# Order edges between bank additions, weight sums and gated sums in a convolutional FFN kernel

## The chip, the cores and the metric

The kernel runs on one core of a Trainium2 chip. Time is device time in microseconds of one launch. Before the change the median of three runs is 2473.03 us (2470.02 to 2473.74).

## The reference

A two-layer decoder on a 1024 x 1024 float32 activation: first an RG-LRU mixer, then a stick-breaking attention, each followed by a convolutional FFN (`D_FF` = 3072) and a layer norm. The change touches the FFN alone:

```python
def causal_depthwise_conv(x, w, b):
    ...
    y = b + xp[:, 0:S] * w[0]
    for k in range(1, K):
        y = y + xp[:, k:k + S] * w[k]
    return y

def conv_ffn(x, w_up, conv_w, conv_b, w_down):
    h = causal_depthwise_conv(x @ w_up, conv_w, conv_b)
    return (jax.nn.gelu(h[..., :D_FF]) * h[..., D_FF:]) @ w_down
```

## The kernel before, in words

**Matmuls.** Every float32 operand is split into a high half (a cast on ACT, tile `whi`, L90) and a low half (a subtraction on POOL, tile `wlo`, L96, on DVE where asked for), and each product takes three matmuls, high by high, high by low, low by high.

**Up projection** (`up`, up to `down` at 866 us in the first layer and at 2213 us in the second). The 24 blocks of 128 hidden units are taken one after the other; block j has a gate half and a value half, 128 x 1024 each. Blocks 0 and 1 are plain. Blocks 2 to 23 use seven half-size products instead of eight (`seven`), with sums of weights (s1 to s4, `combine`, DVE, L467) and sums of the activations made once. PE runs the products in this order: w11 into the bank `cv`, w1 into a bank `p` of its own, w2 on top of w11, w12 into `cg`, then w3, w4, w22. Between them ACT copies banks (L591 `cg<-cv`, L593 `p5s<-p`, L601 `cv<-cv`) and DVE makes two bank additions: c12 (L598, `cg<-cv,p5s`) and c22 (L602, `cv<-cv,p5s`). A product that adds onto such a half waits for its addition. The next block's w11 is started with four matmuls ahead of w3, its other eight stand behind w22.

When both banks are full, `activate` convolves them: ACT scales by the last tap (L483), DVE adds the two other taps in one instruction each (L485), ACT takes the gelu (L491), DVE multiplies the halves (L493, "mul" here).

**Gated sums.** The down projection is also made of seven products for the first 18 blocks. `store(j)` of an odd j makes four sums of the gated halves of the blocks j - 1 and j on POOL (L513, L515, L517, L519) and stores seven half tiles to device memory on SP's queue; it is called while block j + 1 is set up, so the gated sums run in the even blocks 2 to 18. The weight sums and three of the gated sums share one pool tag, `s`, with four buffers. A tag `t2`, four buffers too, is used at the start of the stage alone.

**Down projection** (`down`, `sevens`). Gated half tiles are read back (`graw`, L693, four buffers), weights are loaded (`wr`, L669), the differences T1 to T4 of weights are made on DVE (L675), both operands are split, PE multiplies (L699) and DVE adds the results to the residual `xres` (L650, L653). The first eight operands have their low halves on POOL, of later ones every third is DVE's.

**What sets the order.** A scheduler arranges the instructions of each engine; the engine then runs its list strictly in order, each instruction waiting on semaphores for what it needs. An instruction whose input is ready can so stand behind one that waits. Loads and stores of this stage stand in SP's list, with the same rule. `tc.issue_after(x)` adds an edge: what is issued under it, on x's engine, stands behind x.

Of the kernel before, what the change touches and what calls it, by code (L numbers as in the profile page):

```python
# [7 lines left out]
F32 = mybir.dt.float32  # L8
# [46 lines left out]
def trunk(tc, a):  # L55
# [3 lines left out]
    with ExitStack() as outer:  # L59
# [28 lines left out]
        def split_sb(hi, lo, src, hi_eng="act", lo_eng="pool"):  # L88
            if hi_eng == "act":
                A.copy(out=hi, in_=src)  # L90
            elif hi_eng == "dve":
                V.tensor_copy(out=hi, in_=src)
            else:
                G.tensor_scalar(out=hi, in0=src, scalar1=1.0, scalar2=0.0, op0=ALU.mult, op1=ALU.add)
            eng = G if lo_eng == "pool" else V
            eng.tensor_tensor(out=lo, in0=src, in1=hi.bitcast(F32), op=ALU.subtract)  # L96

# [320 lines left out]
        def ffn(layer, last):  # L418

            gd = [[dram.tile([P, HS], F32, name=f"gs{layer}_{m}_{i}") for i in range(7)] for m in range(NSEV // 2)]  # L420
            gd += [dram.tile([P, S], F32, name=f"gd{layer}_{j}") for j in range(NSEV, NFF)]
            up(layer, last, gd)
            down(layer, last, gd)

        def up(layer, last, gd):
# [6 lines left out]
            with ExitStack() as ph:  # L432
# [18 lines left out]
                def operand(src):  # L451
                    w = Split(ring.tile([P, HS], F32R, name="whi", tag="whi"),
                              ring.tile([P, HS], F32R, name="wlo", tag="wlo"))
                    split_sb(w.hi, w.lo, src)
                    return w

                def blocks(j):

                    out = {}
                    for f, k in ((0, 0), (1, 0), (1, 1), (0, 1)):  # L460
                        raw = out[f, k] = rawp[j % 2].tile([P, HS], F32, name="wraw", tag="wraw")
                        nc.sync.dma_start(out=raw, in_=a["w_up"][layer, f * NFF + j][:, k * HS:(k + 1) * HS])
                    return [out[f, k] for f in range(2) for k in range(2)]
# [25 lines left out]
                def activate(j, pg, pu):  # L489
                    ug = conv(pg, j, "ug", 2)  # L490
                    A.activation(out=ug, in_=ug, func=AF.Gelu_apprx_tanh)  # L491
                    uv = conv(pu, NFF + j, "uv", 1)
                    V.tensor_tensor(out=ug, in0=ug, in1=uv, op=ALU.mult)  # L493
                    done.append(ug)
# [3 lines left out]
                def store(j):  # L498
# [4 lines left out]
                    elif j % 2:  # L503
                        a11, a21, a12, a22 = two(done[j - 1]) + two(done[j])
                        s1, s2, s4 = (sums.tile([P, HS], F32, name="s", tag="s") for _ in range(3))

# [68 lines left out]
                def seven(j, raws):  # L575
                    r11, r12, r21, r22 = raws
                    (b11, b12), (b21, b22) = xq
                    t1, t2, t3, t4 = Ts
                    s1 = combine(ALU.add, r21, r22)
                    s2 = combine(ALU.subtract, s1, r11)  # L580
                    s3 = combine(ALU.subtract, r11, r21)
                    s4 = combine(ALU.subtract, r12, s2)
                    w11, w1, w2, w12, w3, w4, w22 = (operand(r) for r in (r11, s1, s2, r12, s3, s4, r22))
# [17 lines left out]
                    A.copy(out=c21, in_=c22)  # L601
                    V.tensor_tensor(out=c22, in0=c22, in1=p5s, op=ALU.add)  # L602
                    product(c21, w22, t4, False, True)
# [3 lines left out]
                for j in range(NFF):  # L607
                    raws, nxt = nxt, blocks(j + 1) if j + 1 < NFF else None
                    if j in PLAIN:
                        ps = plain(j, raws, None if j else PAIRS if last else (0, 1, 2, 3))  # L610
                        if j == 0:
                            sums_of_x((0, 2, 1))
                    else:
                        ps = seven(j, raws)
                    if j:
                        store(j - 1)
                    activate(j, *ps)
                store(NFF - 1)

        def sevens(layer, gd, ph, banks):  # L620
# [16 lines left out]
            def operand(src, name):  # L637
                w = Split(ring.tile([P, HS], F32R, name=name + "h", tag=name + "h"),
                          ring.tile([P, HS], F32R, name=name + "l", tag=name + "l"))
                turns[0] += 1  # L640
                split_sb(w.hi, w.lo, src, lo_eng="dve" if turns[0] > 8 and turns[0] % 3 == 0 else "pool")
                return w
# [12 lines left out]
            for group, m0 in enumerate(range(0, NSEV // 2, GROUP)):  # L655
                B = {}
                wrp = wrps[group % 2]

                def weight(n, m):
# [6 lines left out]
                    if n in ("11", "12", "21", "22"):  # L666
                        k, d = int(n[0]) - 1, HALVES[int(n[1]) - 1]
                        out = (wfp if n == "11" else wrp).tile([P, HS], F32, name="wr", tag="wr")
                        nc.sync.dma_start(out=out, in_=a["w_down"][layer, (2 * m + k) * P:(2 * m + k + 1) * P, d])  # L669
# [34 lines left out]

        def down(layer, last, gd):
            with ExitStack() as ph:
# [16 lines left out]
                pend = Ends()  # L723
                with ExitStack() as ph7:
                    sevens(layer, gd, ph7, (pmid, pend))
# [323 lines left out]
```

## Time and profile before

| | us |
|---|---|
| median of three runs | 2473.03 |
| the profiled execution, time | 2473.08 |
| its span | 2471.4 |
| layer 0: up projection, blocks 2 to 22 | 435.95 |
| layer 1: the same | 436.92 |

Granted TensorE clock over the span: 0.982 of full speed. The span starts with the RG-LRU mixer; the FFN of layer 0 ends at 1072 us, the attention of layer 1 runs from there to 1713, and its FFN to the end. A row of a timeline gives start and length of an instruction (several of a kind in a row are joined, with xN), and in brackets how long its engine was idle before it and what it waited for. `cv<-Th,whi` is a matmul into bank `cv`.

### The profile page before, as it was taken

Reading aid. Unit: us, or ns where it says so; the run is one execution under the profiler, and the core shown is the slowest. Engines: PE = TensorE matmul, PEld = TensorE weight load, DVE = VectorE, ACT = ScalarE, POOL = GpSimd, SP = SyncE. Lnnn points to the kernel's source line nnn. Section 1 sums busy time; section 2 is a strip of 40 time slices with the busy share of each in tenths; the row PEclk is TensorE's granted clock in tenths of the full one; section 3 lists DMA queues with packets and bytes.
Section 4 is the critical chain, followed back from the end, with each engine's and each line's share of the span. In section 5 each row is a group of like instructions: output and inputs, shape, how many; then the busy total and the mean of one; then the engine's idle time right before and its main releaser. Section 6 shows DMA issues by size and latency. Waiting matters only on the chain.

```text
span 2471.4 us, 29325 instructions
## 1 busy us (share of the span) xinstructions
PE 2306.7 (93%) x10708; PEld 1886.2 (76%) x10708; DVE 1533.0 (62%) x1722; ACT 1004.3 (41%) x1571; POOL 1334.2 (54%) x954
## 2 busy tenths in 40 slices
PE   8999979999999989999999999988999999989998
PEld 6877768777777778888877788767777777768787
DVE  5694756565656578763466555685656565657866
ACT  4644234444444434423433334343444444444441
POOL 4686365565655466764323223246565655456675
PEclk9999989999999999999999999998999999999999
DMA  6111022232322353411011011002222222235351
GB/s 219 47 54 51 18 73 73 81 107 86 105 84 96 106 174 109 147 52 52 26 35 34 26 35 35 26 18 81 77 98 95 93 99 87 90 109 168 103 175 68
DMA packets 95184, 204.52 MB, mean 83 GB/s; under 512 B 10560, under 2 KB 12224, under 8 KB 95040
## 3 DMA queue, kind: packets, MB, share of 16 engines
q1 hardware_dynamic: 90144, 187.74, 23.2%
q10 hardware_dynamic: 4896, 14.92, 1.7%
q8 instruction: 84, 1.38, 0.2%
q14 instruction: 60, 0.49, 0.1%
HBM read 159.10 MB, written 43.52 MB: 82 GB/s over the span
## 4 chain that ended last, share of the span: by engine, by line
PE 56%; DVE 11%; issue 10%; POOL 6%; ACT 1%; DMA 0%; POOLq 0%; DVEq 0%; ACTq 0%
PE cv L475 16%; PE po L699 11%; PE cg L475 5%; PE p L475 5%; DVE s L467 2%; PE pp L114 2%; DVE e L891 2%; PE pp L115 2%; PE pp L116 2%; PE po L153 2%; PE po L154 2%; PE po L157 2%; DVE wr L675 1%; DVE xres L862 1%; POOL s L513 1%
## 5 line engine op out<-in xcount | busy, mean ns | idle before, releaser
L96 POOL TENSOR_TENSOR wlo<-wraw,whi 128x512 fp32r<-128x512 f32 (+2 forms) x217 | 382.4, 1766 | 373.3 <-ACT whi L90 358.1
L96 POOL TENSOR_TENSOR wlo<-s,whi 128x512 fp32r<-128x512 f32 x176 | 233.2, 1330 | 235.8 <-ACT whi L90 183.0
L90 ACT CAST whi<-wraw 128x512 fp32r<-128x512 f32 (+2 forms) x209 | 146.1, 703 | 302.9 <-PE cv L475 126.8
L90 ACT CAST whi<-s 128x512 fp32r<-128x512 f32 x176 | 109.2, 621 | 340.5 <-PE cg L475 117.3
L699 PE MATMUL po<-wh,gh 128*128 128x512 f32 x504 | 198.3, 395 | 23.2 <-DVE ug L485 18.8
L699 PE MATMUL po<-wl,gh 128*128 128x512 f32 x504 | 198.0, 393 | 0.0
L699 PE MATMUL po<-wh,gl 128*128 128x512 f32 x504 | 198.0, 393 | 0.0
L96 POOL TENSOR_TENSOR gl<-graw,gh 128x512 fp32r<-128x512 f32 x86 | 123.9, 1443 | 111.9 <-ACT gh L90 103.7
L475 PE MATMUL cv<-Th,whi 128*128 128x512 f32 x352 | 143.6, 408 | 25.8 <-DVE cg L598 25.3
L475 PE MATMUL cv<-xTh,whi 128*128 128x512 f32 x352 | 139.0, 395 | 25.7 <-DVE cv L602 25.7
L467 DVE TENSOR_TENSOR s<-wraw 128x512 f32<-128x512 f32 x88 | 116.4, 1323 | 70.3 <-POOL wlo L96 67.4
L90 ACT CAST gh<-graw 128x512 fp32r<-128x512 f32 x126 | 78.4, 622 | 190.5 <-PE po L699 68.4
L485 DVE SCALAR_TENSOR_TENSOR ug<-cg,pv,ug 128x1023 f32<-128x1023 f32 x88 | 112.6, 1280 | 49.3 <-ACT ug L483 47.8
L114 PE MATMUL pp<-xTh,whi 128*128 128x512 f32 x352 | 143.1, 406 | 0.0
L475 PE MATMUL cv<-Th,wlo 128*128 128x512 f32 x352 | 137.9, 392 | 0.0
L116 PE MATMUL pp<-xTh,wlo 128*128 128x512 f32 x352 | 137.9, 392 | 0.0
L475 PE MATMUL cv<-Tl,whi 128*128 128x512 f32 x352 | 137.9, 392 | 0.0
L115 PE MATMUL pp<-xTl,whi 128*128 128x512 f32 x352 | 137.8, 391 | 0.0
L475 PE MATMUL cg<-xTh,whi 128*128 128x512 f32 x352 | 137.3, 390 | 0.0
L475 PE MATMUL cg<-xTh,wlo 128*128 128x512 f32 x352 | 137.1, 390 | 0.0
L475 PE MATMUL cv<-xTl,whi 128*128 128x512 f32 x352 | 137.1, 389 | 0.0
L475 PE MATMUL cg<-xTl,whi 128*128 128x512 f32 x352 | 137.0, 389 | 0.0
(254 smaller groups left out, 6448.1 us busy)
## 6 DMA issues: line engine op xcount, KB each, us to landing
wraw<-in_w_up SPq DMA_DIRECT2D x192, 256.0 KB, 2.6
graw<-gs SPq DMA_DIRECT2D x126, 256.0 KB, 2.9
wr<-in_w_down SPq DMA_DIRECT2D x72, 256.0 KB, 4.4
gs<-ug SPq DMA_DIRECT2D x72, 256.0 KB, 2.4
gs<-s SPq DMA_DIRECT2D x54, 256.0 KB, 2.0
wraw<-in_w_in SPq DMA_DIRECT2D x14, 512.0 KB, 3.6
mraw<-gd SPq DMA_DIRECT2D x12, 512.0 KB, 4.3
draw<-in_w_down SPq DMA_DIRECT2D x12, 512.0 KB, 4.5
```

Source lines behind the costliest of these rows:

```text
L90: A.copy(out=hi, in_=src)
L96: eng.tensor_tensor(out=lo, in0=src, in1=hi.bitcast(F32), op=ALU.subtract)
L114: T.matmul(out, lhsT=l.hi, rhs=r.hi, start=start, stop=False)
L115: T.matmul(out, lhsT=l.hi, rhs=r.lo, start=False, stop=False)
L116: T.matmul(out, lhsT=l.lo, rhs=r.hi, start=False, stop=stop)
L153: T.matmul(po[h], lhsT=g.hi, rhs=w.hi[:, d], start=st, stop=False)
L154: T.matmul(po[h], lhsT=g.hi, rhs=w.lo[:, d], start=False, stop=False)
L157: T.matmul(po[h], lhsT=g.lo, rhs=w.hi[:, d], start=False, stop=sp)
L467: V.tensor_tensor(out=s, in0=x, in1=y, op=op)
L475: T.matmul(ps, lhsT=l, rhs=r[:, c, :], start=start and c == k == 0, stop=stop and c == 3 and k == 2, skip_group_check=True)
L485: V.scalar_tensor_tensor(out=u[:, k:], in0=ps[:, :S - k], scalar=cw[:, 2 - k:3 - k], in1=u[:, k:], op0=ALU.mult, op1=ALU.add)
L699: T.matmul(acc[c][t], lhsT=l, rhs=r, start=not on and m == m0 and k == 0, stop=m == m0 + GROUP - 1 and k == 2, skip_group_check=True)
```

## The change

1. `split_sb` returns its last instruction, and `up` keeps a few instructions in `mark`: the last low half, the last load, the last c22, the last mul.
2. The weight sums of a block are issued behind the c22 addition of the block before (an edge on DVE).
3. `store(j - 1)` is issued behind the last low half (POOL) and the last load (SP).
4. The gated sums take tiles of tag `t2`, so that tag `s` has the weight sums and the short use at the start alone.
5. `sevens` is issued behind the last mul. The first twelve operands have their low halves on POOL. The weight pools are dealt out anew: "21" always from one, "12" and "22" from the other in turn.

```diff
@@ -93,7 +93,7 @@
             else:
                 G.tensor_scalar(out=hi, in0=src, scalar1=1.0, scalar2=0.0, op0=ALU.mult, op1=ALU.add)
             eng = G if lo_eng == "pool" else V
-            eng.tensor_tensor(out=lo, in0=src, in1=hi.bitcast(F32), op=ALU.subtract)
+            return eng.tensor_tensor(out=lo, in0=src, in1=hi.bitcast(F32), op=ALU.subtract)
 
         stage = {}
 
@@ -419,8 +419,7 @@
 
             gd = [[dram.tile([P, HS], F32, name=f"gs{layer}_{m}_{i}") for i in range(7)] for m in range(NSEV // 2)]
             gd += [dram.tile([P, S], F32, name=f"gd{layer}_{j}") for j in range(NSEV, NFF)]
-            up(layer, last, gd)
-            down(layer, last, gd)
+            down(layer, last, gd, up(layer, last, gd))
 
         def up(layer, last, gd):
 
@@ -451,15 +450,26 @@
                 def operand(src):
                     w = Split(ring.tile([P, HS], F32R, name="whi", tag="whi"),
                               ring.tile([P, HS], F32R, name="wlo", tag="wlo"))
-                    split_sb(w.hi, w.lo, src)
+                    mark["lo"] = split_sb(w.hi, w.lo, src)
                     return w
+
+
+                mark = {}
+
+                def behind(*names):
+                    order = ExitStack()
+                    for n in names:
+                        if n in mark:
+                            order.enter_context(tc.issue_after(mark[n].ins))
+                    return order
 
                 def blocks(j):
 
                     out = {}
                     for f, k in ((0, 0), (1, 0), (1, 1), (0, 1)):
                         raw = out[f, k] = rawp[j % 2].tile([P, HS], F32, name="wraw", tag="wraw")
-                        nc.sync.dma_start(out=raw, in_=a["w_up"][layer, f * NFF + j][:, k * HS:(k + 1) * HS])
+                        mark["load"] = nc.sync.dma_start(
+                            out=raw, in_=a["w_up"][layer, f * NFF + j][:, k * HS:(k + 1) * HS])
                     return [out[f, k] for f in range(2) for k in range(2)]
 
                 def combine(op, x, y):
@@ -490,7 +500,7 @@
                     ug = conv(pg, j, "ug", 2)
                     A.activation(out=ug, in_=ug, func=AF.Gelu_apprx_tanh)
                     uv = conv(pu, NFF + j, "uv", 1)
-                    V.tensor_tensor(out=ug, in0=ug, in1=uv, op=ALU.mult)
+                    mark["gated"] = V.tensor_tensor(out=ug, in0=ug, in1=uv, op=ALU.mult)
                     done.append(ug)
 
                 done = []
@@ -502,7 +512,7 @@
                         queue.dma_start(out=gd[j - NSEV + NSEV // 2], in_=done[j])
                     elif j % 2:
                         a11, a21, a12, a22 = two(done[j - 1]) + two(done[j])
-                        s1, s2, s4 = (sums.tile([P, HS], F32, name="s", tag="s") for _ in range(3))
+                        s1, s2, s4 = (sums.tile([P, HS], F32, name="t2", tag="t2") for _ in range(3))
 
                         def keep(i, x):
                             nc.sync.dma_start(out=gd[j // 2][i], in_=x)
@@ -576,10 +586,11 @@
                     r11, r12, r21, r22 = raws
                     (b11, b12), (b21, b22) = xq
                     t1, t2, t3, t4 = Ts
-                    s1 = combine(ALU.add, r21, r22)
-                    s2 = combine(ALU.subtract, s1, r11)
-                    s3 = combine(ALU.subtract, r11, r21)
-                    s4 = combine(ALU.subtract, r12, s2)
+                    with behind("c22"):
+                        s1 = combine(ALU.add, r21, r22)
+                        s2 = combine(ALU.subtract, s1, r11)
+                        s3 = combine(ALU.subtract, r11, r21)
+                        s4 = combine(ALU.subtract, r12, s2)
                     w11, w1, w2, w12, w3, w4, w22 = (operand(r) for r in (r11, s1, s2, r12, s3, s4, r22))
                     cv = pcv.tile([P, S], F32, name="cv", tag="cv")
                     c21, c22 = two(cv)
@@ -599,7 +610,7 @@
                     product(c22, w3, t3, False, True)
                     product(c12, w4, b22, False, True)
                     A.copy(out=c21, in_=c22)
-                    V.tensor_tensor(out=c22, in0=c22, in1=p5s, op=ALU.add)
+                    mark["c22"] = V.tensor_tensor(out=c22, in0=c22, in1=p5s, op=ALU.add)
                     product(c21, w22, t4, False, True)
                     return cg, cv
 
@@ -613,9 +624,11 @@
                     else:
                         ps = seven(j, raws)
                     if j:
-                        store(j - 1)
+                        with behind("lo", "load"):
+                            store(j - 1)
                     activate(j, *ps)
                 store(NFF - 1)
+            return mark["gated"]
 
         def sevens(layer, gd, ph, banks):
 
@@ -638,7 +651,7 @@
                 w = Split(ring.tile([P, HS], F32R, name=name + "h", tag=name + "h"),
                           ring.tile([P, HS], F32R, name=name + "l", tag=name + "l"))
                 turns[0] += 1
-                split_sb(w.hi, w.lo, src, lo_eng="dve" if turns[0] > 8 and turns[0] % 3 == 0 else "pool")
+                split_sb(w.hi, w.lo, src, lo_eng="dve" if turns[0] > 4 * GROUP and turns[0] % 3 == 0 else "pool")
                 return w
 
             turns = [0]
@@ -654,7 +667,6 @@
 
             for group, m0 in enumerate(range(0, NSEV // 2, GROUP)):
                 B = {}
-                wrp = wrps[group % 2]
 
                 def weight(n, m):
 
@@ -665,7 +677,8 @@
                         return B[n, m]
                     if n in ("11", "12", "21", "22"):
                         k, d = int(n[0]) - 1, HALVES[int(n[1]) - 1]
-                        out = (wfp if n == "11" else wrp).tile([P, HS], F32, name="wr", tag="wr")
+                        wrp = wfp if n == "11" else wrps[0 if n == "21" else 1 - group % 2]
+                        out = wrp.tile([P, HS], F32, name="wr", tag="wr")
                         nc.sync.dma_start(out=out, in_=a["w_down"][layer, (2 * m + k) * P:(2 * m + k + 1) * P, d])
                     else:
                         x, y, place = {"T1": ("12", "11", "11"), "T2": ("22", "T1", None), "T3": ("22", "12", "12"),
@@ -702,7 +715,7 @@
                         for th, h in into:
                             add(4 * th + t, h, acc[c][t])
 
-        def down(layer, last, gd):
+        def down(layer, last, gd, gated):
             with ExitStack() as ph:
                 def pool(name, **kw):
                     return ph.enter_context(tc.tile_pool(name=f"{name}_d{layer}", reuse_waits="tile", **kw))
@@ -721,7 +734,7 @@
                         return pends[(self.n + 1) // 2 % 2].tile(*args, **kw)
 
                 pend = Ends()
-                with ExitStack() as ph7:
+                with ExitStack() as ph7, tc.issue_after(gated.ins):
                     sevens(layer, gd, ph7, (pmid, pend))
 
                 rawp = pool("raw", bufs=2)
```

**DVE in the steady state.** This is DVE's list before, from the mul of block 3 on; `wraw` is a loaded weight, `s` a weight sum (numbers tell tiles apart), `cg`, `cv` the banks of block 4.

```order
L493 TENSOR_TENSOR ug_3247<-ug_3247,uv_3252 128x1024
L467 TENSOR_TENSOR s_3426<-wraw_3259,wraw_3261 128x512
L467 TENSOR_TENSOR s_3428<-s_3426,wraw_3257 128x512
L598 TENSOR_TENSOR cg_3327<-cv_3301,p5s_3329 128x512
L467 TENSOR_TENSOR s_3430<-wraw_3257,wraw_3259 128x512
L467 TENSOR_TENSOR s_3432<-wraw_3263,s_3428 128x512
L467 TENSOR_TENSOR s_3573<-wraw_3420,wraw_3422 128x512
L467 TENSOR_TENSOR s_3575<-s_3573,wraw_3418 128x512
L602 TENSOR_TENSOR cv_3301<-cv_3301,p5s_3329 128x512
L467 TENSOR_TENSOR s_3577<-wraw_3418,wraw_3420 128x512
L485 SCALAR_TENSOR_TENSOR ug_3408<-cg_3327,pv_66,ug_3408 128x1023
L485 SCALAR_TENSOR_TENSOR ug_3408<-cg_3327,pv_66,ug_3408 128x1022
```

The same place after the change:

```order
L503 TENSOR_TENSOR ug_3247<-ug_3247,uv_3252 128x1024
L609 TENSOR_TENSOR cg_3327<-cv_3301,p5s_3329 128x512
L613 TENSOR_TENSOR cv_3301<-cv_3301,p5s_3329 128x512
L477 TENSOR_TENSOR s_3426<-wraw_3259,wraw_3261 128x512
L477 TENSOR_TENSOR s_3428<-s_3426,wraw_3257 128x512
L477 TENSOR_TENSOR s_3430<-wraw_3257,wraw_3259 128x512
L477 TENSOR_TENSOR s_3432<-wraw_3263,s_3428 128x512
L495 SCALAR_TENSOR_TENSOR ug_3408<-cg_3327,pv_66,ug_3408 128x1023
L495 SCALAR_TENSOR_TENSOR ug_3408<-cg_3327,pv_66,ug_3408 128x1022
L495 SCALAR_TENSOR_TENSOR uv_3413<-cv_3301,pv_66,uv_3413 128x1023
L495 SCALAR_TENSOR_TENSOR uv_3413<-cv_3301,pv_66,uv_3413 128x1022
L503 TENSOR_TENSOR ug_3408<-ug_3408,uv_3413 128x1024
```

Lines of the changed kernel are some ten higher (c12 is L609, c22 L613, weight sums L477). Before, two weight sums stand between mul and c12, four between c12 and c22 and one behind c22, so that this even block has most sums of two blocks. After, c12 and c22 follow mul at once, and four sums stand between c22 and the convolution steps.

**DVE at the transition to the down projection.** Before, from the last c22 on; `wr` and `wt` are weights and their differences, `gl` and `wl` low halves:

```order
L602 TENSOR_TENSOR cv_6202<-cv_6202,p5s_6230 128x512
L675 TENSOR_TENSOR wr_6344<-wr_6512,wr_6344 128x512
L675 TENSOR_TENSOR wr_6512<-wr_6510,wr_6512 128x512
L675 TENSOR_TENSOR wr_6346<-wr_6541,wr_6346 128x512
L675 TENSOR_TENSOR wr_6541<-wr_6539,wr_6541 128x512
L485 SCALAR_TENSOR_TENSOR ug_6296<-cg_6228,pv_66,ug_6296 128x1023
L675 TENSOR_TENSOR wt_6515<-wr_6510,wr_6344 128x512
L485 SCALAR_TENSOR_TENSOR ug_6296<-cg_6228,pv_66,ug_6296 128x1022
L485 SCALAR_TENSOR_TENSOR uv_6301<-cv_6202,pv_66,uv_6301 128x1023
L96 TENSOR_TENSOR gl_6459<-graw_6456,gh_6458 128x512
L485 SCALAR_TENSOR_TENSOR uv_6301<-cv_6202,pv_66,uv_6301 128x1022
L96 TENSOR_TENSOR wl_6485<-wr_6354,wh_6484 128x512
```

After:

```order
L613 TENSOR_TENSOR cv_6202<-cv_6202,p5s_6230 128x512
L495 SCALAR_TENSOR_TENSOR ug_6296<-cg_6228,pv_66,ug_6296 128x1023
L495 SCALAR_TENSOR_TENSOR ug_6296<-cg_6228,pv_66,ug_6296 128x1022
L495 SCALAR_TENSOR_TENSOR uv_6301<-cv_6202,pv_66,uv_6301 128x1023
L495 SCALAR_TENSOR_TENSOR uv_6301<-cv_6202,pv_66,uv_6301 128x1022
L503 TENSOR_TENSOR ug_6296<-ug_6296,uv_6301 128x1024
L96 TENSOR_TENSOR gl_6536<-graw_6533,gh_6535 128x512
L666 SCALAR_TENSOR_TENSOR xres0_75<-xres0_75,po_6356 128x512
L666 SCALAR_TENSOR_TENSOR xres1_76<-xres1_76,po_6357 128x512
L666 SCALAR_TENSOR_TENSOR xres2_77<-xres2_77,po_6358 128x512
L666 SCALAR_TENSOR_TENSOR xres3_78<-xres3_78,po_6359 128x512
L688 TENSOR_TENSOR wr_6344<-wr_6512,wr_6344 128x512
```

The four differences that stood ahead of the first convolution step now stand behind mul and behind four additions to the residual.

**SP's loads at the same place.** Before; `graw` are gated sums read back, `wr_6510` to `wr_6570` the weights from which T1 and T2 of the first group are made:

```order
L669 DMA wr_6510<-in_w_down 128x512
L669 DMA wr_6512<-in_w_down 128x512
L669 DMA wr_6539<-in_w_down 128x512
L669 DMA wr_6541<-in_w_down 128x512
L669 DMA wr_6568<-in_w_down 128x512
L669 DMA wr_6570<-in_w_down 128x512
L669 DMA wr_7448<-in_w_down 128x512
L669 DMA wr_7450<-in_w_down 128x512
L669 DMA wr_7452<-in_w_down 128x512
L693 DMA graw_6456<-gs0_1_1_2339 128x512
L693 DMA graw_6478<-gs0_2_1_2346 128x512
L693 DMA graw_6504<-gs0_0_2_2333 128x512
```

After:

```order
L682 DMA wr_7117<-in_w_down 128x512
L682 DMA wr_7119<-in_w_down 128x512
L706 DMA graw_6456<-gs0_1_1_2339 128x512
L706 DMA graw_6478<-gs0_2_1_2346 128x512
L706 DMA graw_6504<-gs0_0_2_2333 128x512
L706 DMA graw_6533<-gs0_1_2_2340 128x512
L706 DMA graw_6562<-gs0_2_2_2347 128x512
L706 DMA graw_6599<-gs0_0_3_2334 128x512
L706 DMA graw_6621<-gs0_1_3_2341 128x512
L682 DMA wr_6510<-in_w_down 128x512
L682 DMA wr_6512<-in_w_down 128x512
L682 DMA wr_6539<-in_w_down 128x512
```

The loads of the first group's weights stood ahead of the seven `graw` loads and now stand behind them; nine weights of the second group, of which the last two are shown, stand ahead.

## Rows read from the trace of the kernel before

**Rows 1.** The page: TensorE's busy time, and the chain that ended last, by engine.

```profile
PE 2306.7 (93%) x10708; PEld 1886.2 (76%) x10708; DVE 1533.0 (62%) x1722; ACT 1004.3 (41%) x1571; POOL 1334.2 (54%) x954
...
PE 56%; DVE 11%; issue 10%; POOL 6%; ACT 1%; DMA 0%; POOLq 0%; DVEq 0%; ACTq 0%
```

**Rows 2.** Stretches: length; busy us (instructions) of PE, PEld, DVE, ACT, POOL; PEclk; DMA share; GB/s.

```profile
410.21:846.16 435.95, 410.97 (x1781) 330.12 (x1780) 256.10 (x236) 188.44 (x277) 254.77 (x184) 1.00 0.27 93
1756.69:2193.61 436.92, 412.18 (x1781) 331.22 (x1780) 255.00 (x236) 188.55 (x277) 254.10 (x184) 1.00 0.27 93
517.05:536.34 19.29, 19.29 (x85) 15.69 (x84) 9.21 (x9) 9.07 (x15) 9.54 (x8) 1.00 0.17 54
536.34:558.90 22.56, 19.66 (x85) 15.61 (x84) 15.37 (x14) 8.75 (x13) 15.75 (x12) 1.00 0.37 129
410.21:433.36 23.15, 21.56 (x102) 17.22 (x100) 16.94 (x18) 9.88 (x16) 15.47 (x12) 1.00 0.35 126
787.36:846.16 58.80, 58.67 (x253) 46.84 (x252) 32.33 (x32) 26.72 (x40) 27.07 (x22) 1.00 0.22 73
872.00:878.00 6.00, 4.81 (x11) 3.84 (x12) 6.00 (x7) 1.57 (x2) 2.22 (x2) 0.50 0.29 98
```

**Rows 3.** Waits of PE, 407 to 866: sum, count, longest (us).

```profile
PE cv L475 <- DVE cv L602: 13.7, 9, 1.6
...
PE cv L475 <- DVE cg L598: 12.0, 10, 1.4
```

**Rows 4.** Timeline of PE in an even block: start, length, instruction, idle before it.

```profile
547.17 0.50 PE L475 MATMUL cv<-Th,whi 128*128 128x512 f32 x1 [1.37 <-DVE cg L598]
...
554.44 0.50 PE L475 MATMUL cv<-xTh,whi 128*128 128x512 f32 x1 [1.54 <-DVE cv L602]
```

**Rows 5.** Timeline of DVE in that block.

```profile
545.81 0.69 DVE L467 TENSOR_TENSOR s<-s,wraw 128x512 f32<-128x512 f32 x1 [3.79 <-POOL s L517]
...
546.42 0.69 DVE L598 TENSOR_TENSOR cg<-cv,p5s 128x512 f32<-128x512 f32 x1
...
548.92 1.76 DVE L467 TENSOR_TENSOR s<-wraw 128x512 f32<-128x512 f32 x1 [1.81 <-POOL wlo L96]
...
551.21 1.77 DVE L467 TENSOR_TENSOR s<-wraw 128x512 f32<-128x512 f32 x1
...
553.70 0.69 DVE L602 TENSOR_TENSOR cv<-cv,p5s 128x512 f32<-128x512 f32 x1
```

**Rows 6.** Timeline of POOL in that block.

```profile
541.42 1.75 POOL L513 TENSOR_TENSOR s<-ug 128x512 f32<-128x512 f32 x1
...
545.86 1.78 POOL L519 TENSOR_TENSOR s<-ug,s 128x512 f32<-128x512 f32 x1
...
547.59 2.55 POOL L96 TENSOR_TENSOR wlo<-s,whi 128x512 fp32r<-128x512 f32 x2
```

**Rows 7.** Timeline of ACT, then DVE, at the end of the odd block before it.

```profile
529.63 0.58 ACT L601 COPY cv<-cv 128x512 f32<-128x512 f32 x1
...
537.77 0.58 ACT L591 COPY cg<-cv 128x512 f32<-128x512 f32 x1
...
533.61 2.60 DVE L485 SCALAR_TENSOR_TENSOR ug<-cg,pv,ug 128x1023 f32<-128x1023 f32 x2 [2.66 <-ACT ug L483]
```

**Rows 8.** From up to down projection: DVE, PE, SP's queue; the page's issues of wr.

```profile
862.16 6.79 DVE L675 TENSOR_TENSOR wr<-wr 128x512 f32<-128x512 f32 x4 [2.46 <-POOL wl L96]
...
885.60 2.48 DVE L653 SCALAR_TENSOR_TENSOR xres<-xres,po 128x512 f32<-128x512 f32 x4
...
873.19 0.77 PE L699 MATMUL po<-wh,gh 128*128 128x512 f32 x1 [9.39 <-DVE ug L485]
...
892.03 0.39 PE L699 MATMUL po<-wh,gh 128*128 128x512 f32 x1
...
860.90 23.06 SPq L693 DMA_DIRECT2D graw<-gs  x7
...
wr<-in_w_down SPq DMA_DIRECT2D x72, 256.0 KB, 4.4
```


## The prediction

> **What bounds the kernel now.** I read the page first: PE is busy for 93% of the span and leads the chain that ended last, with DVE second at 11% [rows 1]. So only time in which PE stands can go. Then a row for each stretch: in both convolutional FFNs' up projections the clock is granted in full (1.00), and PE is busy 410.97 of 435.95 us and 412.18 of 436.92 [rows 2]. These two stretches are the blocks j = 2 to 22 of each layer, from the first matmul of product p of one block to that of the next. A block of seven products is 84 matmuls. An odd block shows what they take with nothing in the way: 19.29 us, PE busy throughout, 0.2296 a matmul. An even block, in which the gated sums run, takes 22.56 with PE busy 19.66 [rows 2]. There are 8 such even ones in a layer (j = 4 to 18); one of layer 1's is longer, whence its extra 1.0.
>
> The waits give the names: in layer 0 PE waits for bank addition c22 (L602) 13.7 us and for c12 (L598) 12.0 [rows 3]; layer 1 has the same two rows. In the timeline an even block loses 1.37 before product w12 and 1.54 before the next w11 [rows 4]. Each stop also costs a restart: 22.56 - 19.29 = 3.27 against 2.91 of waits.
>
> DVE in that block tells why. The c12 addition is ready early but stands behind a weight sum, which waits 3.79 for POOL's gated sum L517: both share four buffers of tag s. Then the weight sums stand ahead of c22: the first waits 1.81 for a low half of POOL, and two run 1.76 and 1.77 where others take 0.69, so c22 begins at 553.70 [rows 5]. POOL is at the gated sums from 541.42 to 547.6, and at low halves behind them [rows 6]. PE waits for DVE's queue order, not for DVE's work.
>
> **The change, part by part.** *Weight sums behind c22, gated sums in t2.* Nothing is computed more or less. DVE now has mul, c12, c22, then s1 to s4, then the four convolution steps. c12 waits for PE's bank alone, and so does c22, apart from the copy c21 ahead of it. Both PE waits should go in every even block, and the restarts with them.
>
> What is late next? In the odd block c21's copy starts at 529.63, the convolution steps at 533.61, and the copy c11 (L591) at 537.77, ending 538.35 [rows 7]. The second product, of w2, starts 12 matmuls after 536.34, at 539.1, and needs that copy. Now four additions stand between c22 and the convolution steps. The copy c21 goes ahead of the cast of w1 and so ends by 530.0 instead of 530.2; c22 follows and ends near 530.6. At the pitch of 0.6 (545.81 to 546.42 [rows 5]) four take 2.4; if one meets a POOL low half it takes 1.08 more (1.77 against 0.69). They end near 534.1, 0.5 later than the steps now begin. Steps 2.60, gelu (now behind the cast of w22), copy c11, which stands right behind gelu and no longer behind a cast: it ends near 538.6. That is 0.5 before it is wanted, so I cost the four additions at nothing, hidden by PE's products w3 to p; without that cover each further contended addition costs 1.08 a block, less the 0.5.
>
> The prices of additions at this place are not shown before, so bounds: none contended, 0; all four contended, 3 x 1.08 - 0.49 = 2.75 a block. I take one: in rows 5 some weight sums run at 0.69 beside a POOL that is fed one operand at a time, and here s1 begins while POOL makes the low half of w11; that of w1 can't begin before s1 and its cast are done, when two of the other three have run.
>
> The low half of w1 gets later too: s1 ends near 531.2, cast 0.6, low half 1.3 behind it, so near 533.7; PE wants it for the third matmul of p, at 536.8. Hidden, with 3 us left. In the even blocks POOL's gated sums (6.2 us [rows 6]) start when mul ends and are done some 2 us before the next c22, so low halves don't meet them. The stores stand behind the block's loads on SP; behind them are the loads of a later block, whose buffers come free a block later than the stores land. Nothing either way.
>
> So each of 20 blocks at 19.29, and the first, with 16 transposes, at its busy 21.56 [rows 2]: 407.36. Layer 0: 435.95 - 407.36 = 28.6; layer 1: 436.92 - 407.36 = 29.6. In this stand about 0.9 for three blocks of layer 0 without gated sums (58.80 against 57.87 [rows 2]), and as much in layer 1, which may stay. Together **58.2**.
>
> *Down stage behind the last gated product.* Now DVE makes four weights (862.16, 6.79) ahead of the convolution steps, and PE's first down product waits 9.39 for them [rows 8]. After it, the steps come first: they could end at 865, but the second matmul needs a low half of POOL, whose eighth operation it now is: 859.6 + 8 x 1.29 = 869.9, so PE starts near 870 and not 873.19. Granted clock there is 0.50 (1.2 GHz) behind a gap of some 10 us [rows 2]; I leave it. But the differences T1 and T2 now stand behind the additions to the residual: 885.60 + 2.48 [rows 8], 3.2 earlier as PE starts earlier, 884.9. The third operation is T2's first operand; six of them 0.6 apart end near 888.5, cast 0.62 and low half 1.30 make 890.4 to 890.7. PE wants it 18.84 after its start (873.19 to 892.03 [rows 8]), at 888.9. So it begins at about 890.7 against 892.0: **1.2** saved a layer. Bounds: 7.9 saved if only the steps count (865.3 to 873.2), 5.1 lost if the loads decide (below). I take 1.2, since each link has a row. Sum: 58.2 + 2.4 = 60.6. The profiled run took 2473.08, 0.05 above the median: **2412.5**.
>
> **A rule against it.** The row says: four DVE additions beside POOL's low halves took 6.79, 1.70 each [rows 8], so both engines alternate. The Trainium skill, SBUF — State Buffer, "SBUF: two separate sides", calls the port pair that VectorE and GpSimd share an exclusive lock that whichever starts first holds for its whole instruction. That agrees with the row. By it, four additions moved to where POOL makes low halves would each wait out one POOL instruction; that is the first rival, priced by the row.
>
> **Rivals.**
> 1. *All, or three, of the additions meet POOL in every block.* Then copy c11 is late and PE waits for ACT cg instead. 42 blocks x 2.75 = 115: 2528, slower. With three: 42 x 1.67 = 70: 2483. The point from which it is slower than before is 60.6 / 42 = 1.44 a block. For: 6.79 for four [rows 8]. Against: POOL has two low halves at most between c22 and the steps, 530 to 534, and two additions of rows 5 ran alone.
> 2. *Two meet POOL:* 42 x 0.59 = 25: 2437.
> 3. *The down stage pays for its order.* Loads of the operands for T1 and T2 stand behind seven loads of gated sums, which now take 23.06 from 860.90 [rows 8], since they wait for buffers. Then: 884.0, six loads 2.7, landing 4.4 [rows 8], six additions 4.1, cast and low half 1.9: 897.1 against 892.0, 5.1 lost a layer: 2473.08 - 58.2 + 10.2 = 2425. Against: the seven wait for low halves that POOL now makes without pause.
> 4. *The waits stay.* POOL's order is nearly the same, the gated sums still stand between low halves of w11 and w1, and if c12 waited for those it would not matter where it stands: 2470. Against: the waits of rows 5 are DVE's own, behind weight sums.
>
> **How the numbers follow.** Forecast 0.56, rival 2 0.16, rival 3 0.13, rival 4 0.05, rival 1 0.08, an unnamed gain of the down stage (to 2399) 0.02. Low end: 7.9 saved a layer would be 2399; I take 2401. High end 2440, which holds rivals 2 and 3 and leaves out 1 and 4 (0.13). Changes of 0.2% (4.9 us) and less can't be told from none. Faster: forecast, 2, 3 and the unnamed, 0.87; rival 4, mostly same: 0.04; slower 0.09, for rival 1 and the odd 0.01.
>
> **What would show it.** Right: every block between two p starts at 19.3; waits for c12 and c22 gone from PE; DVE c12, c22, then four additions with one at 1.7; copy c11 done before 539.1 in that block's clock; PE's first down matmul earlier by some 3 us. Wrong: PE rows "<-ACT cg" (rivals 1, 2), several weight sums at 1.7, a wait for wt or wr behind the first 72 down products (rival 3), or c12 still late behind POOL (rival 4).

## The result, and the profile after

The changed kernel takes 2410.28 us (median of four, 2408.71 to 2411.81) against 2473.39 of the kernel before, a ratio of 0.9747 [0.973, 0.9764]. 2412.5 was forecast. Its profiled execution has a span of 2407.7 us and a granted clock of 0.981. The page's busy line and chain of work that ended last, which answer to [rows 1]:

```profile
PE 2300.2 (96%) x10708; PEld 1889.0 (78%) x10708; DVE 1537.8 (64%) x1718; ACT 994.0 (41%) x1571; POOL 1374.5 (57%) x958
...
PE 45%; DVE 9%; issue 7%; POOL 2%; DMA 1%; ACT 1%; SPq 0%; POOLq 0%; DVEq 0%; ACTq 0%
```

PE does the same 10708 matmuls in a span 63.7 us shorter, busy for 96% of it; POOL has 2% of the chain instead of 6%. The stretches that answer to [rows 2] (same columns) are blocks 2 to 22 of both layers, an even block with its gated sums, and the way from the last block's product p to the first wait for a residual addition in the down stage ("the way" below):

```profile
408.72:816.17 407.45, 407.14 (x1782) 331.05 (x1780) 254.29 (x235) 183.49 (x276) 267.56 (x182) 1.00 0.29 98
1724.50:2131.99 407.49, 407.18 (x1781) 331.06 (x1780) 254.26 (x235) 183.46 (x276) 267.54 (x182) 1.00 0.29 98
526.33:545.63 19.30, 19.30 (x85) 15.69 (x84) 12.07 (x12) 8.67 (x14) 15.80 (x12) 1.00 0.41 138
816.17:911.08 94.91, 85.57 (x362) 69.13 (x360) 70.61 (x76) 38.75 (x67) 67.75 (x47) 0.95 0.51 164
```

The even block that took 22.56 takes 19.30, like an odd one. The two up projections lost 435.95 - 407.45 = 28.5 and 436.92 - 407.49 = 29.4. Of PE's waits in [rows 3], 25.7 us together, one row of 1.2 is left in layer 0, and most of it is a wait of 0.86 in the last block that the kernel before has too:

```profile
PE cv L485 <- DVE cg L609: 1.2, 2, 0.9
```

The same way in the kernel before:

```profile
846.16:942.25 96.09, 84.74 (x362) 69.06 (x360) 67.56 (x77) 38.86 (x66) 59.40 (x43) 0.95 0.48 156
```

Here 96.09 - 94.91 = 1.2 went; in layer 1 (2193.61 to 2290.05 before, 2131.99 to 2226.44 after) it was 2.0. Together 57.9 + 3.2 = 61.1 of the 63.7. The other 2.6 lie outside the edited stretches, 1.5 ahead of block 2 of layer 0 and 1.0 between the stretches of the two layers; the stretch ahead of block 2 takes 407.6 to 412.3 in the runs below, and four runs of one kernel spread over 3 to 4 us.

DVE in an even block, the place of [rows 5]:

```profile
534.76 0.70 DVE L609 TENSOR_TENSOR cg<-cv,p5s 128x512 f32<-128x512 f32 x1 [3.23 <-PE cg L485]
...
539.18 0.70 DVE L613 TENSOR_TENSOR cv<-cv,p5s 128x512 f32<-128x512 f32 x1 [3.73 <-ACT cv L612]
...
539.79 0.68 DVE L477 TENSOR_TENSOR s<-wraw 128x512 f32<-128x512 f32 x1
...
541.17 0.68 DVE L477 TENSOR_TENSOR s<-wraw 128x512 f32<-128x512 f32 x1
...
541.77 1.78 DVE L477 TENSOR_TENSOR s<-wraw,s 128x512 f32<-128x512 f32 x1
...
543.48 2.59 DVE L495 SCALAR_TENSOR_TENSOR ug<-cg,pv,ug 128x1023 f32<-128x1023 f32 x2
```

c12 now waits for PE's bank alone, and c22 for ACT's copy. Three weight sums run at 0.68 to 0.69, and the last, s4, at 1.78. POOL, the place of [rows 6]:

```profile
536.63 1.29 POOL L529 TENSOR_TENSOR t<-ug,t 128x512 f32<-128x512 f32 x1
...
541.26 3.46 POOL L96 TENSOR_TENSOR wlo<-s,whi 128x512 fp32r<-128x512 f32 x2 [3.34 <-PE cg L485]
```

The gated sums are done before c22. POOL then waits 3.34 for the cast of s1, which ends at 541.18; the row names PE, but with the edge behind c22 alone (below) the same wait names the cast. Its low half of w1 lengthens s4 and no other sum. ACT's copy c11 of the block before, and PE's product of w2 that needs it ([rows 7] show the same copy before the change):

```profile
527.83 0.58 ACT L602 COPY cg<-cv 128x512 f32<-128x512 f32 x1
```

```profile
529.05 0.39 PE L485 MATMUL cv<-Th,whi 128*128 128x512 f32 x1
```

The copy ends at 528.41, 0.64 before 529.05. PE at the transition to the down projection ([rows 8]):

```profile
835.48 0.47 PE L712 MATMUL po<-wh,gh 128*128 128x512 f32 x1 [1.67 <-ACT uv L493]
...
840.59 0.79 PE L712 MATMUL po<-wl,gh 128*128 128x512 f32 x1 [4.64 <-POOL wl L96]
...
860.93 0.50 PE L712 MATMUL po<-wl,gh 128*128 128x512 f32 x1 [1.04 <-POOL wl L96]
```

PE's first down product starts at 835.48, but its second matmul waits 4.64 for POOL's eighth low half, and a later one 1.04 for that of T2. The eighth low half runs beside DVE's mul and takes 2.25, where the seven ahead of it take 1.28 to 1.29:

```profile
838.28 2.25 POOL L96 TENSOR_TENSOR wl<-wr,wh 128x512 fp32r<-128x512 f32 x1
```

DVE makes T1 and T2 late:

```profile
838.09 1.33 DVE L503 TENSOR_TENSOR ug<-ug,uv 128x1024 f32<-128x1024 f32 x1
...
851.33 0.69 DVE L96 TENSOR_TENSOR gl<-graw,gh 128x512 fp32r<-128x512 f32 x1 [11.91 <-ACT gh L90]
...
855.13 0.81 DVE L688 TENSOR_TENSOR wr<-wr 128x512 f32<-128x512 f32 x1 [0.71 <-DMA wr<-in_w_down]
...
857.25 0.69 DVE L688 TENSOR_TENSOR wr<-wr 128x512 f32<-128x512 f32 x1 [1.30 <-DMA wr<-in_w_down]
```

DVE is idle for 11.91 behind mul, adds to the residual, and then waits 0.71 and 1.30 for loads that stood behind seven loads of gated sums.

### The profile page after: what moved, and what is told of

It reads as the page before. It is cut to its first block, busy times and chain, and to the rows that moved or that the text cites. A ratio compares the mean times of both kernels' runs of the same rounds, so it can differ in the third digit from the quotient of the medians.

```text
span 2407.7 us, 29186 instructions
## 1 busy us (share of the span) xinstructions
PE 2300.2 (96%) x10708; PEld 1889.0 (78%) x10708; DVE 1537.8 (64%) x1718; ACT 994.0 (41%) x1571; POOL 1374.5 (57%) x958
## 4 chain that ended last, share of the span: by engine, by line
PE 45%; DVE 9%; issue 7%; POOL 2%; DMA 1%; ACT 1%; SPq 0%; POOLq 0%; DVEq 0%; ACTq 0%
PE cv L485 10%; PE po L712 10%; PE cg L485 5%; PE p L485 2%; PE pp L114 2%; PE pp L115 2%; PE pp L116 2%; DVE e L904 2%; PE po L153 2%; PE po L154 2%; PE po L157 2%; DVE wr L688 1%; DVE xres L875 1%; DVE b L905 1%; PE pp L135 1%
## 5 line engine op out<-in xcount | busy, mean ns | idle before, releaser
L96 POOL TENSOR_TENSOR wlo<-wraw,whi 128x512 fp32r<-128x512 f32 (+2 forms) x217 | 401.2, 1860 | 224.4 <-ACT whi L90 209.0
L96 POOL TENSOR_TENSOR wlo<-s,whi 128x512 fp32r<-128x512 f32 x176 | 265.0, 1527 | 300.5 <-PE cg L485 260.1
L612 ACT COPY cv<-cv 128x512 f32<-128x512 f32 x44 | 25.1, 570 | 363.3 <-PE cv L485 363.3
L485 PE MATMUL cv<-xTh,wlo 128*128 128x512 f32 x352 | 136.9, 389 | 0.0
```

The lines of the kernel that those rows point to most:

```text
L96: return eng.tensor_tensor(out=lo, in0=src, in1=hi.bitcast(F32), op=ALU.subtract)
L485: T.matmul(ps, lhsT=l, rhs=r[:, c, :], start=start and c == k == 0, stop=stop and c == 3 and k == 2, skip_group_check=True)
```

## The experiments

**The parts of the change.** The four kernels of this part are compared with the same runs of the kernel before (2473.97).

*The up projection's edits alone*: the changed kernel with the down stage as before.

```diff
-                with ExitStack() as ph7, tc.issue_after(gated.ins):
+                with ExitStack() as ph7:
-  ... turns[0] > 4 * GROUP and turns[0] % 3 == 0 ...
+  ... turns[0] > 8 and turns[0] % 3 == 0 ...
-  ... wrps[0 if n == "21" else 1 - group % 2]
+  ... wrps[group % 2]
```

> The three edits of the up projection (weight sums behind c22, gated sums in t2, stores behind the loads), the down projection as before. My theory, that the gain is PE's waits for c12 and c22 in the up projection: 58 us below before, near 2415, every block at 19.3, the first down product 9.4 late as before. Rival, that a good part comes from the down stage: above 2425.

Measured 2413.04, ratio 0.9754 [0.9741, 0.9767]: nearly all of the gain. The way takes 95.24 and 95.25, so the down edits bring 0.3 and 0.8 on top, not the 1.2 and 2.0 by which the kernels before and after differ. PE's late start is back:

```profile
842.13 0.76 PE L712 MATMUL po<-wh,gh 128*128 128x512 f32 x1 [9.40 <-DVE ug L495]
```

*The down stage's edits alone.*

```diff
-                    with behind("c22"):
+                    with behind():
-                        with behind("lo", "load"):
+                        with behind():
-  ... sums.tile([P, HS], F32, name="t2", tag="t2") ...
+  ... sums.tile([P, HS], F32, name="s", tag="s") ...
```

> The down stage behind the last gated product, its low halves and its weight pools, as in the changed kernel; the up projection as before. My theory: the gain from the last block to the first wait for a residual addition in the changed kernel, 1.2 us in layer 0 and 2.0 in layer 1, stays: 2470, even blocks at 22.5. Rival, that only the better up projection lets the down stage start well: no gain, 2473 or more.

Measured 2471.44, ratio 0.9991 [0.9982, 1.0]: 2.5 us less, no more than can be told from none. In the trace the way is 94.31 and 95.18 long against 96.09 and 96.44 before, 1.8 and 1.3 less, and the even blocks keep their waits of 1.37 and 1.54.

*The edge behind c22 alone*: from the kernel with the up edits alone,

```diff
-                        with behind("lo", "load"):
+                        with behind():
-  ... sums.tile([P, HS], F32, name="t2", tag="t2") ...
+  ... sums.tile([P, HS], F32, name="s", tag="s") ...
```

> Only the edge that puts weight sums behind c22; gated sums share tag s with the weight sums, down stage as before. DVE's order in the blocks is then that of the changed kernel. My theory, that the order is what matters and the gated sums' buffers are free again when the weight sums want them: as the kernel with all three up edits, 2415, within 5. Rival, that own buffers are needed: the last weight sum waits for the stores in 16 even blocks, 1 to 2 us each: 2430 to 2447.

Measured 2415.07, ratio 0.9759 [0.9746, 0.9773]. From block 3 on every block but one (20.35, in layer 1) is at 19.3 here too, so the edge alone takes the waits away. The own buffers add nothing that can be seen once the edge is there: the weight sums run without a wait for a buffer, the last one too:

```profile
505.55 0.69 DVE L477 TENSOR_TENSOR s<-s,wraw 128x512 f32<-128x512 f32 x1
...
506.16 0.69 DVE L477 TENSOR_TENSOR s<-wraw 128x512 f32<-128x512 f32 x1
...
506.76 1.78 DVE L477 TENSOR_TENSOR s<-wraw,s 128x512 f32<-128x512 f32 x1
```

The edge of the stores was not run by itself: without it each engine's list comes out the same, so it does nothing here.

*Own buffers alone*: from the same kernel,

```diff
-                    with behind("c22"):
+                    with behind():
-                        with behind("lo", "load"):
+                        with behind():
```

> Only own buffers for the gated sums; no edges, down stage as before. The scheduler then gives DVE the order mul, s1, c12, s2, c22, s3, two convolution steps, s4. My theory: the wait of a weight sum for a gated sum goes, but sums that wait for POOL's low halves still stand ahead of c12 and c22: between, 2430 to 2465. Rival, that sharing the buffers was the whole cause: 2415.

Measured 2554.34, ratio 1.0325 [1.0309, 1.0341]: slower than before, which neither theory had. DVE in an even block:

```profile
504.98 2.15 DVE L503 TENSOR_TENSOR ug<-ug,uv 128x1024 f32<-128x1024 f32 x1
...
513.70 1.73 DVE L477 TENSOR_TENSOR s<-wraw 128x512 f32<-128x512 f32 x1 [6.57 <-POOL wlo L96]
...
515.36 0.69 DVE L609 TENSOR_TENSOR cg<-cv,p5s 128x512 f32<-128x512 f32 x1
```

With more buffers the scheduler takes the weight sums of the next block but one ahead, and puts the first of them right before c12. It waits 6.57 for POOL's low halves, and these stand behind the gated sums. c12 is late in every even block, here so that PE waits 5.45 for it, and the clock falls behind the gap:

```profile
501.04:528.50 27.46, 21.96 (x86) 17.27 (x85) 12.03 (x12) 8.89 (x13) 13.96 (x12) 0.88 0.28 96
516.00:522.00 6.00, 5.90 (x16) 4.66 (x17) 0.64 (x2) 0.76 (x2) 0.06 (x1) 0.58 0.00 0
```

The block takes 27.46. The granted clock over six us behind the gap is 0.58, so most of them ran at 1.2 GHz, the lower of the two levels. More buffers without a stated order moved the wrong work forward.

**The cover of the additions.** s4 is made once or twice more in every block, between c22 and the convolution steps:

```diff
                         s4 = combine(ALU.subtract, r12, s2)
+                        V.tensor_tensor(out=s4, in0=r12, in1=s2, op=ALU.subtract)
```

> The changed kernel with the last weight sum s4 made twice in every block, so that a fifth addition stands between c22 and the convolution steps. POOL is at low halves without a pause there, so it should take about 1.7 like the fourth. Copy c11 now ends 0.64 before PE's product of w2 starts. My theory, that this copy is the next thing late: 1.70 - 0.64 = 1.06 a block, 42 blocks, 45 us: 2455, waits of PE for ACT cg. Rival, that the additions have much more cover than that: 2410 to 2415.

Measured 2464.83, ratio 0.9973 [0.9961, 0.9984]. The fifth addition took 1.67, and PE waits for the copy c11:

```profile
509.87 1.79 DVE L477 TENSOR_TENSOR s<-wraw,s 128x512 f32<-128x512 f32 x1
...
511.69 1.67 DVE L594 TENSOR_TENSOR s<-wraw,s 128x512 f32<-128x512 f32 x1
```

```profile
517.57 0.50 PE L485 MATMUL cv<-Th,whi 128*128 128x512 f32 x1 [0.95 <-ACT cg L603]
```

The mechanism is the one expected. The size was 0.2 short: blocks take 20.56, 1.26 more, of which 0.95 is the wait and 0.31 the restart, left out of the expectation. (A row's wait counts from the end of a matmul of 0.39, while PE otherwise starts one every 0.23; about half of the 0.31 is that, the rest the slower starts behind the stop.) 42 x 1.26 = 53.

> The same with s4 made three times: a fifth and a sixth addition. My theory, the price that rival 1 of the prediction gave to contended additions: 3.4 - 0.64 = 2.76 a block, 116 us, 2526, slower than the kernel before. Rival: the sixth runs alone at 0.6 and the blocks stretch so that POOL and DVE meet less: 2470 to 2490.

Measured 2483.28, ratio 1.0046 [1.0033, 1.006], slower than before by less than 0.5%. The rival's range holds, and the sixth addition took 0.68. But it did not run alone. The scheduler put it between two convolution steps, a low half of POOL began beside it, and POOL was the one that took longer, 1.83 where others take 1.28:

```profile
513.71 1.67 DVE L594 TENSOR_TENSOR s<-wraw,s 128x512 f32<-128x512 f32 x1
...
515.30 1.27 DVE L495 SCALAR_TENSOR_TENSOR ug<-cg,pv,ug 128x1023 f32<-128x1023 f32 x1
...
516.50 0.68 DVE L595 TENSOR_TENSOR s<-wraw,s 128x512 f32<-128x512 f32 x1
...
516.49 1.83 POOL L96 TENSOR_TENSOR wlo<-s,whi 128x512 fp32r<-128x512 f32 x1
```

Blocks take 21.03, 1.73 more; 42 x 1.73 = 73. The prediction called the change slower from 1.44 a block on. The two runs stand on either side of that: 1.26 a block is still a little faster than before, 1.73 a little slower.

**What is left at the transition.** The wait of 4.64 comes from the order of POOL's low halves. Three kernels changed the order of the products instead.

*21 ahead of 11 in the first group:*

```diff
-  ... in ((0, "11", 0, False, ((0, 0),)), (1, "21", 1, False, ((0, 0),)), ...
+  ... in (*(((0, "11", ...), (1, "21", ...)) if group else ((1, "21", ...), (0, "11", ...))), ...
```

> The changed kernel with the products of weight 21 ahead of those of weight 11 in the first group of the down stage, so that PE's first down product wants POOL's first low halves and not the seventh and eighth. My theory: the wait of 4.64 for a low half goes and the clock stays up with it, but the additions that make T2 stand behind the residual additions and their loads behind seven loads of gated sums, which come earlier only as PE does: 4 to 5 a layer, 2401. Rival, the loads decide alone: no gain, 2409 to 2411.

*The same, with the pools swapped:*

```diff
-  ... wrps[0 if n == "21" else 1 - group % 2]
+  ... wrps[0 if n == "21" else group % 2]
```

> The same, and the two weight pools swapped for 12 and 22, so that the first group's weights for T1 and T2 are loaded ahead of the second group's. Their additions then stand ahead of the residual additions on DVE, in a stretch of 11.9 us in which DVE is idle in the changed kernel. My theory: the waits of 4.64 and 1.04 go, and the slow matmuls behind the gap, 12 at about 0.43: 7 to 8 a layer, 2395. Rival, POOL's low halves bound the start anyway: 2403 or more.

*21, 11, T1, T2, with T3 and T4 behind the residual additions* (the pools as in the kernel before this; `hold` is the last residual addition of the first two products):

```diff
+                if not group:
+                    steps = [steps[k] for k in (1, 0, 3, 2, 4, 5, 6)]
...
-                        V.tensor_tensor(out=out, in0=x, in1=y, op=ALU.subtract)
+                        with tc.issue_after(hold[0].ins) if n in ("T3", "T4") and group == 0 else ExitStack():
+                            V.tensor_tensor(out=out, in0=x, in1=y, op=ALU.subtract)
```

> A version meant to beat the changed kernel: in the first group of the down stage the products run in the order 21, 11, T1, T2, so that PE's first wants POOL's first low halves, no product adds onto a bank whose residual addition is only just due, and T1 needs one addition and not two; pools as in e10; the additions for T3 and T4 stand behind the residual additions of the first two products. My theory: 72 matmuls after its start at 835.5 PE would reach the third product at 852 instead of 860.9, and half of these 9 us a layer stay: 2400. Rival, that a wait of some 5 us only moves on, as in e9 and e10: 2409 to 2415.

Measured 2412.81 (ratio 0.9765 [0.9752, 0.9778]), 2422.67 (0.9803 [0.9789, 0.9816]) and 2413.39 (0.976 [0.9745, 0.9774]). None is faster than the changed kernel. In each the wait of 4.64 went and a longer one came later. The first rival named the cause rightly, the loads, and the third the size; the second did not, since POOL's low halves no longer bound the start there. PE's next long wait in the three, in this order:

```profile
858.74 0.76 PE L714 MATMUL po<-wh,gh 128*128 128x512 f32 x1 [5.50 <-ACT wh L90]
```

```profile
862.43 0.77 PE L714 MATMUL po<-wh,gh 128*128 128x512 f32 x1 [11.23 <-DVE xres L663]
```

```profile
874.88 0.77 PE L720 MATMUL po<-wh,gh 128*128 128x512 f32 x1 [6.67 <-DVE xres L666]
```

In the first, DVE waits 6.48 for a load before it can make T1 and T2:

```profile
853.10 0.69 DVE L688 TENSOR_TENSOR wr<-wr 128x512 f32<-128x512 f32 x1 [6.48 <-DMA wr<-in_w_down]
```

In the other two a residual addition stands on DVE behind differences of weights that run at 1.7 beside POOL; in the last:

```profile
863.69 5.19 DVE L691 TENSOR_TENSOR wr<-wr,wt 128x512 f32<-128x512 f32 x3
...
868.80 1.75 DVE L96 TENSOR_TENSOR gl<-graw,gh 128x512 fp32r<-128x512 f32 x1
...
870.47 1.87 DVE L666 SCALAR_TENSOR_TENSOR xres<-xres,po 128x512 f32<-128x512 f32 x3
```

*The gated-product edge without the new pools and low halves:*

```diff
-  ... turns[0] > 4 * GROUP and turns[0] % 3 == 0 ...
+  ... turns[0] > 8 and turns[0] % 3 == 0 ...
-  ... wrps[0 if n == "21" else 1 - group % 2]
+  ... wrps[group % 2]
```

> The changed kernel with the weight pools and the first low halves of the down stage as before, so that of its edits there only the edge behind the last gated product is left. DVE then takes two low halves and the additions for T1 and T2 in the 11.9 us in which it is idle in the changed kernel. My theory: the wait of 1.04 for a low half goes, the 4.64 at the start stays, since the eighth low half is POOL's either way: 2408. Rival, the additions meet POOL's low halves at 1.7 each and delay them: 2412 to 2415.

Measured 2407.56, ratio 0.974 [0.9727, 0.9754]. The interval overlaps with that of the changed kernel; the traces tell them apart: the way is 93.60 and 92.96 against 94.91 and 94.45, together 2.8 less, and the wait of 1.04 is gone, while one of 4.65 at the start stays. DVE uses the stretch in which it was idle:

```profile
839.18 1.75 DVE L96 TENSOR_TENSOR gl<-graw,gh 128x512 fp32r<-128x512 f32 x1
...
842.54 2.37 DVE L688 TENSOR_TENSOR wr<-wr 128x512 f32<-128x512 f32 x2
...
844.83 1.28 DVE L688 TENSOR_TENSOR wt<-wr 128x512 f32<-128x512 f32 x2
```

Against the kernel with the up edits alone the edge brings 3.9 (1.64 and 2.29), and the other two edits, which were not run one by one, take 2.8 of it back.

*This kernel, with the first two operand pairs of 21 loaded and split ahead of those of 11:*

```diff
+                def load(i, n, m):
+                    raw = rawp.tile([P, HS], F32, name="graw", tag="graw")
+                    nc.sync.dma_start(out=raw, in_=gd[m][i])
+                    return operand(raw, "g"), operand(weight(n, m), "w")
+                early = {(1, m): load(1, "21", m) for m in range(m0, m0 + 2) if not group}
...
-                        raw = rawp.tile([P, HS], F32, name="graw", tag="graw")
-                        nc.sync.dma_start(out=raw, in_=gd[m][i])
-                        g = operand(raw, "g")
-                        w = operand(weight(n, m), "w")
+                        g, w = early.pop((i, m), None) or load(i, n, m)
```

> The kernel with the old pools and low halves of the down stage (the run before this one, 2407.6), and in the first group the first two operand pairs of the product of weight 21 loaded and split ahead of those of weight 11. The order of PE's products stays, since two banks are free for 21 first; only POOL's first low halves are now those that PE wants first. My theory: the wait of 4.65 goes, PE runs on from 835.3 with POOL ahead of it, and the slow clock behind the gap with it: 4.5 to 7 a layer, 2394 to 2399. Rival, the wait moves on to a later low half or a residual addition, as when the products were put in another order: 2405 or more.

Measured 2397.41 (2396.76 to 2399.79), ratio 0.9701 [0.9687, 0.9714], the fastest of these kernels and as expected. PE:

```profile
838.21 0.47 PE L715 MATMUL po<-wh,gh 128*128 128x512 f32 x1 [1.67 <-ACT uv L493]
...
864.90 0.47 PE L715 MATMUL po<-wh,gh 128*128 128x512 f32 x1 [1.54 <-DVE xres L663]
```

It waits 1.67 once and then runs without a stop; a new wait of 1.54 for a residual addition is the price. The granted clock of the stretch:

```profile
830.00:842.00 12.00, 10.33 (x46) 8.25 (x45) 7.01 (x6) 9.97 (x16) 9.68 (x8) 1.00 0.60 194
842.00:850.00 8.00, 8.00 (x37) 6.64 (x36) 8.00 (x7) 0.94 (x2) 6.42 (x4) 1.00 0.50 165
```

It stays at 1.00, where the changed kernel had 0.55 behind its gap:

```profile
841.00:847.00 6.00, 6.00 (x16) 4.65 (x16) 0.00 (x0) 0.00 (x0) 4.49 (x4) 0.55 0.43 147
```

Up to the residual wait that ended the way in the other kernels (here it is the second), the way is 88.15 and 88.17, together 10.2 less than in the kernel that it was made from, and the medians differ by 10.15.

## Why the prediction was right

**The sum.** 407.36 was worked out for 21 blocks; 407.45 and 407.49 came out. Two small errors cancel in it: the first block took 21.11 and not 21.56, the twenty others 386.3 and not 385.8. For the down stage 2.4 was forecast and 3.2 came. The total was 2.2 us too high, within what runs spread.

**PE's waits go.** This was right, and it is shown by the run with the edge alone. What was not seen is that own buffers do nothing beside the edge and, alone, cost 80 us. The prediction had priced the edge and the buffers as one step.

**One of four additions meets POOL.** The count was right, half of the reason wrong, so the count is luck in part. s1 was to meet the low half of w11, but POOL stands idle there. The other half holds: w1's low half can't begin before s1 and its cast, and by then the third sum has begun (541.17 against 541.26). The third still takes 0.68; s4 behind it pays.

**Copy c11 next.** It was forecast to end 0.5 ahead of its need, and measured 0.64; one more addition made it the bound, as rivals 1 and 2 have it. Their price left out a restart of about 0.3 a stop. The prediction had read one for the old waits (0.36 for two stops, [rows 2, 4]) but did not put it on new ones.

**Low half of w1.** 3 us of cover were forecast (the terms given, 531.2, 0.6 and 1.3, make 533.1 and not 533.7, so 3.7). The first of the two low halves at 541.26 ends near 543, and p's third matmul is at 546.1: 3.1.

**Down stage.** PE's start near 870 of the old clock of the trace was forecast, bound by POOL's eighth low half. It is: the second matmul, at 840.59, is 870.6 there (the starts of the last p lie 29.99 apart). T2's wait was to be 1.8 and is 1.04, but that step came out by luck. It counted six additions at 0.6 between the residual additions and T2's first cast, and left the loads to rival 3. Three additions stand there, and the other 2.0 are the waits of 0.71 and 1.30 for the loads. So rival 3 is there in small, and the pools and low halves together cost 2.8.

That the down edits bring 1.2 a layer is not shown. Alone they took 1.8 and 1.3 off the way, on top of the up edits 0.3 and 0.8. The kernel with the up edits alone has a way 0.8 and 1.2 shorter than before, although its wait at the start is as long; its slow matmuls end sooner (last section).

## What to carry to other kernels

Where an in-order engine makes a bank addition that a product waits for, state what may stand ahead of it; here waits that named that engine were those of an instruction queued ahead. Before such an order is filled up with more work, count the time between its end and the next thing due: here it was 0.64 us, and one contended addition used it up in every block. At a change of stage, see which operand PE takes first and let the engine that is behind make that one first: here this brought 10 us, and three ways of moving PE's products brought nothing.

## What the runs showed of the hardware

A DVE addition of two SBUF tiles took 0.68 to 0.69 alone and 1.67 to 1.79 beside a POOL addition or subtraction, which took 1.28 to 1.30 alone. The Trainium skill, SBUF — State Buffer, "SBUF: two separate sides", has the shared ports locked by one for its whole instruction; that one waits for the other agrees with these rows. Not every pair costs DVE: the third weight sum took 0.68 although POOL's low half began during it, and the sixth addition too; there the low halves took 1.75 and 1.83. A pair's lengths add up to 0.68 + 1.29 = 1.97, and 1.67 to 1.79 was measured; but rows of one engine overlap by about 0.1 too (DVE's third sum is 0.68 long and the fourth starts 0.60 behind its start), so this does not show that the two ran side by side.

The granted clock stayed at 1.00 behind a PE gap of 1.67. It was 0.55 over six us in the changed kernel, where one matmul stands between a gap of 1.67 and one of 4.64, and 0.58 behind a gap of 5.45. Equal gaps did not give equal slow stretches. Behind gaps of 9.4 the clock over 12 us was 0.79 and 0.75 in the two layers of the kernel before, and 0.86 in both with the up edits alone, which makes about 0.8 and 1.3 us that no edit explains. In the changed kernel it was 0.76 and 0.83 in the two layers, so a good part of the difference between the 1.2 and the 2.0 is the clock's.
